# The norm after each expert: passes into a tile of its own, small products four steps late, 14 weight slots instead of 15

## The chip, the cores and the metric

One Trainium2 chip, one NeuronCore of it. The metric is the device time of one execution in microseconds (us). The time before is 2308.57 us, the median of 3 runs (2307.85 to 2309.63).

## The reference, cut to what matters

```
h = concat(meta, x)                       # 16 + 1024 tokens of 2048
h = layer_norm(h, ln_in_g, ln_in_b)       # the input norm
mix = hybrid_mixer(h, ...)                # input projection, convolution and pooling heads, output projection
h = layer_norm(ALPHA*h + mix, ln_mix_g, ln_mix_b)
# mixture of experts: every token goes to 2 of 32 experts
y[t] = sum over its two experts e of gate[t, e] * (silu(h[t] @ w_gate[e]) * (h[t] @ w_up[e])) @ w_down[e]
out  = layer_norm(ALPHA*h + y, ln_ffn_g, ln_ffn_b)[16:]

def layer_norm(x, g, b):
    mu = mean(x); xc = x - mu
    return xc * rsqrt(mean(xc * xc) + 1e-5) * g + b      # over the 2048 columns of a row
```

Each expert has 12 MB of weights (w_gate and w_up 2048x512 each, w_down 512x2048, float32), 32 experts 384 MB.

## The kernel before, in words

The first part (to about 1084 us) normalises the input rows, projects them with float32 numbers that are split into a high and a low half (three products for one), runs the convolution and the pooling, projects the result and routes every token. `ln_stats`, `ln_aggr`, `ln_scale` and `ln_block` are the input norm, on two or three tiles of 128 rows at a time (`PAIRS`); `ln_step` spreads the norm of the next pair over the steps of the present one. Its `aggr` makes mean and reciprocal root on DVE, in fourteen small operations (a bit trick and three Newton steps, all at L262).

The second part (from about 1084 us) goes through the 32 experts in a fixed order. Tokens are sorted by expert; an expert's rows stand in blocks of 32, 64, 96 or 128 rows. A block of up to 64 rows is **narrow** (tile `xgn`): each row is folded over 4 (32 rows) or 2 (64 rows) groups of partitions, so that the block fills 128 partitions. A **wide** block (tile `xgw`) has a row in a partition. An expert has 16 G steps (gate and up products, `gu`) and 8 D steps (down products, `down`). Its weights are 12 units of 1 MB; a step uses half a unit. The list `steps` interleaves experts: the first 8 G steps of the next expert stand ahead of the D steps of this one. SP issues the loads of the units into a ring of 15 slots (10 `er`, 3 `e2a`, one `e2c`, one `e2d`); a slot is loaded again when its unit has been used.

In the step loop each step issues its matmuls (L1482 records all of them), then one advance of what is spread over steps:

- `chain`: the generator `hidden` of the expert whose G steps have ended. ACT makes silu and copies the up sums, DVE multiplies (`sg`, L1572), `YX` = 3 steps later PE transposes `sg` (L1578), and the D steps use it (`hth`). For a 32-row part DVE first adds two halves (`od`, L1502).
- `x_next`: PE transposes of the next expert's rows (L1537), copied to `xt` or `xn` by DVE or ACT (L1539).
- `norm_next`: one advance of the norm at the head of the queue `norms`.

At an expert's last D step `y_out` adds the sums to the block's rows (L1599, L1604, L1615, L1617). Then `rows_out` calls `send` (POOL writes the partial rows to `yd`, L1412), queues the block's norm, sets DVE's `flags` of the next expert (L1636 to L1650) and, `PVS` = 2 steps later, `sums_in` fetches the next expert's partial rows.

`norm`, the function most changed, is on DVE: `bn_stats` (L1668), `bn_aggr` (L1671), then for a narrow block two small products on PE that join the groups of partitions of a row: the mean with `lmv` (L1680) and the variance with `lve` (L1687), each `MATMUL ms<-..,pc`. PE takes its instructions in order, so a step's weight matmuls behind a small product wait with it. Behind it come eight Newton operations and eight **passes** over 512 columns each, in pairs: L1709 takes off the mean and multiplies by the gain, L1710 multiplies by the reciprocal root and adds the offset, both in place in `xgw` or `xgn`. POOL then scatters the block's rows to the output (`out_dram`, L1412). An advance of the norm does one pair of passes, and passes wait until `LNS` = 7 steps behind `rows_out`. A block's place (`xg`) is free for the gather of a later block 8 steps behind the norm's end. The very last norm (`gb` given) has its rows folded by four, so that two passes (L1702, L1703) do it.

Of the kernel before, what the change touches and what calls it, by code (L numbers as in the profile page):

```python
# [57 lines left out]
NE2 = {"a": 3, "c": 1, "d": 1}  # L58

FIRST, FIRST2 = ("a", "a", "a", "c", "d", "x"), ("er", "er", 0, 1)  # L60
# [19 lines left out]
PVS, LNS = 2, 7  # L80
# [3 lines left out]
def trunk_kernel(ctx, tc, xcat, gin, bin_, grow, brow, w_in, b_in, conv_w, conv_b, cln_g, cln_b,  # L84
# [208 lines left out]

    def ln_aggr(tiles):
        c0, c1 = CI[tiles[0]], CI[tiles[-1]] + 1
        aggr([LST[i] for i in tiles], xstat[:, 0, c0:c1], xstat[:, 1, c0:c1])
# [379 lines left out]
    def ln_step(n, g):  # L676
        if n == 0:
# [4 lines left out]
        f = g * 8 // len(GROUPS[n])  # L682
        if (g + 1) * 8 % len(GROUPS[n]) or n + 1 == len(PAIRS):
            return
        nx = PAIRS[n + 1]
        if f == 0:
            ln_stats(nx[-2])
        elif f == 2:
            if nx[0] == 0:
                ln_stats(0)  # L690
            ln_stats(nx[-1])
        elif f == 4:
            ln_aggr(nx)
        elif f in (5, 6, 7):
            for c in ((0,), (1,), (2, 3))[f - 5]:
                ln_scale(nx, c)
# [15 lines left out]
    ln_aggr((1, 2))  # L712
    T0 = []
# [634 lines left out]
    e2["d"] = pool("e2d", NE2["d"])  # L1348
# [6 lines left out]
    lnp = pool("lnp", 3)  # L1355
# [149 lines left out]
    class Block:  # L1505


        def __init__(self, start, n):
            self.start, self.n = start, n
# [45 lines left out]
        def hidden(self):  # L1555
# [12 lines left out]
            for part, (g_, u_) in both.items():  # L1568
# [61 lines left out]
        def flags(self):  # L1630
# [11 lines left out]
            v.scalar_tensor_tensor(ix[:m, 1:2], es[:m], -float(NONE), ef[:m, 1:2], op0=OP.mult, op1=OP.add)  # L1642
            if self.f == 1:
# [15 lines left out]
        def norm(self, into=None, gb=None, wait=lambda: True, idx=None):  # L1659

            f, v = self.f, nc.vector
            m, nseg = self.m if f == 1 else P, 4 // f
            xg, y = self.xg, self.xg if into is None else into
# [3 lines left out]
            for c in range(nseg):  # L1667
                v.bn_stats(out=st[:m, c, :], in_=xg[:m, c * 512:(c + 1) * 512])  # L1668
                if c % 2:
                    yield  # L1670
# [5 lines left out]
            else:  # L1676

                yield
# [5 lines left out]
                yield  # L1684
                yield
# [8 lines left out]
            yield  # L1694
            for _ in range(3):
                v.scalar_tensor_tensor(y2, r, nv, r, op0=OP.mult, op1=OP.mult)
                v.scalar_tensor_tensor(r, y2, 1.5, r, op0=OP.add, op1=OP.mult)
            yield
            while not wait():
                yield  # L1700
            if gb is not None:
                v.scalar_tensor_tensor(xg[:, :512], xg[:, :512], nm, gb[0], op0=OP.add, op1=OP.mult)  # L1702
                v.scalar_tensor_tensor(y[:, :512], xg[:, :512], r, gb[1], op0=OP.mult, op1=OP.add)  # L1703
            else:
                for c in range(4):
# [3 lines left out]
                    v.scalar_tensor_tensor(xg[pc, xc], xg[pc, xc], rs[pc, 0:1], lfg[pc, cs], op0=OP.add, op1=OP.mult)  # L1709
                    v.scalar_tensor_tensor(y[pc, xc], xg[pc, xc], rs[pc, 1:2], lfb[pc, cs], op0=OP.mult, op1=OP.add)  # L1710
                    yield
# [14 lines left out]
    next_ent, next_gather = [0], [0]  # L1726
# [124 lines left out]
    for b in POS[0]:  # L1851
        b.flags()
# [11 lines left out]
    now, norms, sums = [0], deque(), deque()  # L1864

    def rows_out(p, n):
# [3 lines left out]
        for b in POS[p]:  # L1870
            b.send()
            t = er_tile() if last else None
            if last:
                assert b.f == 4
            norms.append((b, b.norm(t, (FIN[:, :512], FIN[:, 512:1024]) if last else None,
                                    lambda: last or now[0] >= n + LNS)))
        nc.vector.tensor_scalar(lim[:, r:r + 1], base[:, r:r + 1],
                                float(FBLK[1] if p < len(STAT) else sum(BLOCKS[RANK[p]][-1])), None, op0=OP.add)
        if not last:
            for b in POS[p + 1]:  # L1880
                b.flags()
# [10 lines left out]
    for n, (kind, p, k) in enumerate(steps):  # L1892
        now[0] = n
        while sums and sums[0][0] <= n:
            for b in POS[sums.popleft()[1]]:
                b.sums_in()
# [3 lines left out]
        if kind == "G":  # L1900
# [16 lines left out]
            if k == 15:  # L1917
                while todo:
                    x_next()
                chain.extend((p, b.hidden()) for b in POS[p])  # L1920
# [30 lines left out]
        norm_next()  # L1951
# [5 lines left out]
    while len(norms) > 1:  # L1957
        norm_next()
    while norms:
        norm_next()  # L1960
# [8 lines left out]
    def left_out(it):  # L1969
# [4 lines left out]
        blk = Block(st, P)  # L1974
        blk.en, blk.xg, blk.gb, blk.pds = ent_load(e, st, P), SPARE, PB6[:2], [PB6[2:4], PB6[4:]]
# [3 lines left out]
    with tc.For_i(0, nov, 1) as it:  # L1979
        blk, e = left_out(it)  # L1980
        blk.fetch()
        blk.flags()
# [87 lines left out]
```

## Time and profile before

| what | value |
|---|---|
| median of 3 runs | 2308.57 us (2307.85 to 2309.63) |
| the profiled execution: time / span | 2310.51 / 2308.7 us |
| busy in the span: PE (matmul) | 2053.9 us (89%) |
| PEld (weight loads of PE) | 1187.8 us (51%) |
| DVE / ACT / POOL | 1414.9 (61%) / 652.8 (28%) / 695.3 us (30%) |
| mean granted clock of PE | 0.943 |
| moved by DMA | 606.52 MB, mean 263 GB/s |
| loads of 1 MB weight units, issue to landing | about 10 us each (median of a group) |

A busy PE is one that has matmuls in it, at whatever clock: the granted clock is given beside it, 1.00 for 2.4 GHz. A wait is idle time of an engine, put down to the instruction on another engine, or the DMA, that ended it. The shares are means over very different stages, so the rows below are read by stage. The profiled execution lasted 1.94 us longer than the median of the runs, and 1.81 us longer than its own span.

### The profile page before, as it was taken

The numbers are of one execution on the slowest core, as the hardware profiler recorded it, in microseconds if no ns is written. First come the engines' busy times: TensorE is split into PE (matmuls) and PEld (weight loads), VectorE is DVE, ScalarE is ACT, GpSimd is POOL, SyncE is SP. The second block draws the span as 40 slices with busy tenths as digits, with TensorE's granted clock in tenths as the row PEclk, the third lists the DMA queues.
The fourth block names the chain that finished last, engine by engine and source line by source line (L and its number), as shares of the span: only waits on it lengthen the run. The fifth ranks groups of instructions, "written<-read, shape, count | busy, mean of one in ns | idle before, by whom it ended". The sixth has DMA issues, their size and how long they took to land. (4 is left out here: it accounts for less than half of the span.)

```text
span 2308.7 us, 30565 instructions
## 1 busy us (share of the span) xinstructions
PE 2053.9 (89%) x10899; PEld 1187.8 (51%) x10899; DVE 1414.9 (61%) x2975; ACT 652.8 (28%) x1159; POOL 695.3 (30%) x593
## 2 busy tenths in 40 slices
PE   5899999999999989985789998989878999788993
PEld 4799999978877878764222222223222232222321
DVE  8678677768675795797375536563554354526445
ACT  5634343423343453543111211121111112111111
POOL 5566657635122354374111101110111011101101
PEclk8999999999999999998899999989988999899996
DMA  6211121133667866677999988996899999978992
GB/s 208 90 55 56 56 65 55 56 97 114 213 210 271 277 216 201 225 273 270 410 394 409 391 311 337 402 412 254 351 359 419 407 361 410 403 278 317 388 386 105
DMA packets 141740, 606.52 MB, mean 263 GB/s; under 512 B 29353, under 2 KB 36009, under 8 KB 87477
## 3 DMA queue, kind: packets, MB, share of 16 engines
q1 hardware_dynamic: 122432, 554.11, 63.3%
q0 software_dynamic: 17712, 42.03, 4.9%
q10 hardware_dynamic: 1440, 8.39, 0.9%
q8 instruction: 87, 1.43, 0.3%
q14 instruction: 69, 0.57, 0.1%
HBM read 579.68 MB, written 73.51 MB: 283 GB/s over the span
## 5 line engine op out<-in xcount | busy, mean ns | idle before, releaser
L760 PE MATMUL mm<-hl,whi 128*128 128x256 f32 (+2 forms) x1152 | 359.4, 324 | 0.6 <-POOL hl L349 0.6
L759 PE MATMUL mm<-hh,whi 128*128 128x256 f32 (+2 forms) x1152 | 347.3, 326 | 0.4 <-ACT l L595 0.4
L379 POOL TENSOR_TENSOR wlo<-raw,whi 128x512 fp32r<-128x512 f32 x129 | 175.4, 1360 | 397.2 <-ACT whi L378 336.9
L1482 PE MATMUL mm<-er,xt 128*64 128x512 f32 (+1 forms) x1248 | 272.3, 642 | 0.0
L764 PE MATMUL mm<-hh,wlo 128*128 128x256 f32 (+2 forms) x1152 | 257.9, 323 | 1.9 <-POOL wlo L379 1.8
L378 ACT ACTIVATE whi<-raw 128x512 fp32r<-128x512 f32 x252 | 156.7, 627 | 270.2 <-PE mm L760 132.7
L418 DVE SCALAR_TENSOR_TENSOR ms<-l,cwt,ms 128x512 f32<-128x512 f32 x352 | 232.5, 747 | 0.0
L760 PEld LDWEIGHTS mm<-hl,whi 128*128 128x128 f32 x1152 | 218.9, 190 | 18.7 <-POOL hl L349 1.0
L759 PEld LDWEIGHTS mm<-hh,whi 128*128 128x128 f32 x1152 | 219.2, 190 | 3.4 <-ACT l L595 0.8
L764 PEld LDWEIGHTS mm<-hh,wlo 128*128 128x128 f32 x1152 | 193.6, 190 | 36.9 <-POOL wlo L379 2.8
L1482 PE MATMUL mm<-er,hth 128*64 128x512 f32 (+1 forms) x1016 | 194.6, 619 | 0.0
L1482 PE MATMUL mm<-er,xn 128*64 128x512 f32 (+1 forms) x840 | 168.3, 646 | 1.2 <-DVE xn L1539 1.2
L1240 PE MATMUL mm<-wlo,yh 128*128 128x512 f32 x392 | 157.6, 402 | 8.3 <-DVE wlo L379 8.2
L1239 PE MATMUL mm<-whi,yh 128*128 128x512 f32 x392 | 159.8, 408 | 0.3 <-ACT whi L378 0.3
L1241 PE MATMUL mm<-whi,yl 128*128 128x512 f32 x392 | 156.5, 399 | 0.0
L1482 PEld LDWEIGHTS mm<-er,xt 128*64 128x64 f32 (+1 forms) x1248 | 68.0, 134 | 162.2 <-issue 159.1
L1615 DVE SCALAR_TENSOR_TENSOR xgw<-mm,xgw 64x512 f32<-64x512 f32 x44 | 30.2, 687 | 191.4 <-ACT dt L1614 190.4
L434 POOL TENSOR_TENSOR l<-l,t 128x512 f32<-128x512 f32 x112 | 142.0, 1298 | 0.0
L379 DVE TENSOR_TENSOR wlo<-raw,whi 128x512 fp32r<-128x512 f32 x123 | 104.5, 861 | 58.4 <-ACT whi L378 56.7
L1482 PEld LDWEIGHTS mm<-er,hth 128*64 128x64 f32 (+1 forms) x1016 | 53.9, 130 | 136.5 <-issue 130.5
L1599 DVE SCALAR_TENSOR_TENSOR xgn<-mm,xgn 64x512 f32<-64x512 f32 x40 | 27.5, 688 | 156.1 <-ACT dt L1597 155.8
L1482 PE MATMUL mm<-e2a,xt 128*64 128x512 f32 (+1 forms) x448 | 97.7, 623 | 0.0
(350 smaller groups left out, 3186.1 us busy)
## 6 DMA issues: line engine op xcount, KB each, us to landing
er<-in_w_gu_dram SPq DMA_DIRECT2D x168, 1024.0 KB, 10.2
er<-in_w_dn_dram SPq DMA_DIRECT2D x86, 1024.0 KB, 10.0
e2a<-in_w_gu_dram SPq DMA_DIRECT2D x54, 1024.0 KB, 10.7
raw<-in_w_out_dram SPq DMA_DIRECT2D x70, 512.0 KB, 5.0
raw<-in_w_in_dram SPq DMA_DIRECT2D x56, 512.0 KB, 3.3
e2a<-in_w_dn_dram SPq DMA_DIRECT2D x21, 1024.0 KB, 9.9
e2d<-in_w_gu_dram SPq DMA_DIRECT2D x17, 1024.0 KB, 11.1
t<-in_xcat_dram SPq DMA_DIRECT2D x56, 256.0 KB, 6.1
```

The source lines that it names most:

```text
L378: nc.scalar.activation(h, src, AF.Copy)
L379: self.lo(s).tensor_tensor(l, src, fr(h), op=OP.subtract)
L418: nc.vector.scalar_tensor_tensor(a, src, w, a, op0=OP.mult, op1=OP.add)
L434: nc.gpsimd.tensor_tensor(a, a, t, op=OP.add)
L759: nc.tensor.matmul(o, wh[:, ks], hh[q][:, kk, a0:a1], start=k == 0, stop=False)
L760: nc.tensor.matmul(o, wh[:, ks], hl[q][:, kk, a0:a1], start=False, stop=False)
L764: nc.tensor.matmul(o, wl[:, ks], hh[q][:, kk, a0:a1], start=False, stop=k == 15)
L1239: nc.tensor.matmul(po[t_], a_, wh, start=n == 0, stop=False)
L1240: nc.tensor.matmul(po[t_], a_, wl, start=False, stop=False)
L1241: nc.tensor.matmul(po[t_], b_, wh, start=False, stop=n == 15)
L1482: nc.tensor.matmul(bank[c:c + self.n], lhs(h_)[:, self.r0:self.r0 + self.n], t[:, h_ * 1024 + j * 512:h_ * 1024 + (j + 1) * 512], start=fi ...
L1615: nc.vector.scalar_tensor_tensor(xs, y0, a, xs, op0=OP.mult, op1=OP.add)
```

## The change

- Input norm: the reciprocal root comes from ACT's square root, a DVE reciprocal and one Newton step (new `ln_rstd`), and ACT copies the mean; in `ln_step` both now stand ahead of the step's own evacuation of sums.
- The weight ring loses slot `e2d` (15 to 14 slots); its 8 KB a partition become `lnz`, a tile for the norm.
- The norm's first passes read the block and write `lnz`, the second passes work in `lnz`, and the scatter reads `lnz`. All four first passes come ahead of the four second ones, one pass an advance. The block's place is free 3 steps behind the last first pass. The wait for `LNS` is gone.
- The small products of a narrow block are issued `PRS` = 4 steps behind the operation before them, both of them (0 for the last expert).
- `norm_next` advances up to two norms in turns (the second one only while the first counts its steps), rests while an expert's `sg` has not been issued, and issues the flags in three portions; the fetch of sums is `PVS` = 4 steps behind `rows_out`.

```diff
-NE2 = {"a": 3, "c": 1, "d": 1}
+NE2 = {"a": 3, "c": 1}
-FIRST, FIRST2 = ("a", "a", "a", "c", "d", "x"), ("er", "er", 0, 1)
+FIRST, FIRST2 = ("a", "a", "a", "c", "x"), ("er", "er", 0, 1)
-PVS, LNS = 2, 7
+PVS, PRS = 4, 4
...
+        nc.scalar.activation(sd, mv[:, :, 1], AF.Sqrt, bias=epst)
+        nc.scalar.activation(xstat[:, 0, c0:c1], mv[:, :, 0], AF.Copy)
+        nc.vector.tensor_scalar(ve, mv[:, :, 1], EPS, -0.5, op0=OP.add, op1=OP.mult)
+        LMV[tiles[0]] = ve, sd, xstat[:, 1, c0:c1]
+
+    def ln_rstd(tiles):
+        ve, sd, rs = LMV.pop(tiles[0])
+        nc.vector.reciprocal(rs, sd)
+        nc.vector.tensor_tensor(sd, rs, rs, op=OP.mult)
+        nc.vector.tensor_tensor(sd, sd, ve, op=OP.mult)
+        nc.vector.scalar_tensor_tensor(rs, sd, 1.5, rs, op0=OP.add, op1=OP.mult)
...
+        if nx and f == 4:
+            ln_aggr(nx)
+        if nx and f == 5:
+            ln_rstd(nx)
         if n == 0:
             ln_evac(PAIRS[0], *GROUPS[0][g], T0[g])
...
-    e2["d"] = pool("e2d", NE2["d"])
+    lnz = pool("lnz", 1).tile([P, D], F32, name="lnz")
...
             nc.vector.scalar_tensor_tensor(sg[:m], sg[:m], self.en[:m, 2:3].bitcast(F32), ul[:m],
                                            op0=OP.mult, op1=OP.mult)
+            self.gated = True
...
-                yield
+                yield from until(now[0] + lag)
                 p_ = ms()
                 nc.tensor.matmul(p_[:, 0:1], PIECE[f], mv[:, 0:1], start=True, stop=True)
...
-                yield
-                yield
+                yield from until(now[0] + lag)
                 q_ = ms()
...
-            while not wait():
-                yield
...
-                for c in range(4):
+                for turn, c in [(t_, c) for t_ in range(2) for c in range(4)]:
...
-                    v.scalar_tensor_tensor(xg[pc, xc], xg[pc, xc], rs[pc, 0:1], lfg[pc, cs], op0=OP.add, op1=OP.mult)
-                    v.scalar_tensor_tensor(y[pc, xc], xg[pc, xc], rs[pc, 1:2], lfb[pc, cs], op0=OP.mult, op1=OP.add)
-                    yield
+                    if not turn:
+                        v.scalar_tensor_tensor(y[pc, xc], xg[pc, xc], rs[pc, 0:1], lfg[pc, cs], op0=OP.add, op1=OP.mult)
+                    else:
+                        v.scalar_tensor_tensor(y[pc, xc], y[pc, xc], rs[pc, 1:2], lfb[pc, cs], op0=OP.mult, op1=OP.add)
+                    if (turn, c) == (0, 3):
+                        sent[self.place] = now[0]
+                    yield True
...
-            if sent.get(b.place, -99) + 8 > n or b.f == 1 and n < WSTEP:
+            if sent.get(b.place, -99) + 3 > n or b.f == 1 and n < WSTEP:
...
     def norm_next():
-        if norms and next(norms[0][1], 0) == 0:
-            sent[norms.popleft()[0].place] = now[0]
+        if marks:
+            mark_next()
+        for g in list(norms)[:2]:
+            r = next(g[1], None)
+            if r is None:
+                norms.remove(g)
+            if r is not False:
+                return
...
-        norm_next()
+        if all(c[2].gated for c in chain):
+            for _ in range(1 + (len(norms) > 2)):
+                norm_next()
```

Place 1 is PE's order of instructions at the end of the thirteenth expert (one block of 32 rows; the products on `xt` and `xn` are those of the next expert, with blocks of 128 and 64 rows). `hth` are the last D steps. Before:

```order
L1482 MATMUL mm<-er,hth 32x512 x16
L1482 MATMUL mm<-er,xt 64x512 x4
L1482 MATMUL mm<-er,xn 64x512 x2
L1680 MATMUL ms<-lmv,pc_10490 128x1
L1482 MATMUL mm<-er,xt 64x512 x4
L1482 MATMUL mm<-er,xn 64x512 x2
```

After the change:

```order
L1507 MATMUL mm<-er,hth 32x512 x16
L1507 MATMUL mm<-er,xt 64x512 x4
L1507 MATMUL mm<-er,xn 64x512 x2
L1507 MATMUL mm<-er,xt 64x512 x4
L1507 MATMUL mm<-er,xn 64x512 x2
L1507 MATMUL mm<-er,xt 64x512 x4
L1507 MATMUL mm<-er,xn 64x512 x2
L1507 MATMUL mm<-er,xt 64x512 x4
L1507 MATMUL mm<-er,xn 64x512 x2
L1562 MATMUL ms<-ident,xgn_10332 128x128 x4
L1713 MATMUL ms<-lmv,pc_10453 128x1
```

Between the D end and the first small product stood the matmuls of one step, now those of four steps and a transpose. (The trace counts each of these matmuls twice.)

Place 2 is DVE's order ahead of `sg` of a 32-row expert, the 24th; the norm there is that of the 23rd, a wide block of 96 rows. Before, from the last copy of rows on:

```order
L1709 SCALAR_TENSOR_TENSOR xgw_10344<-xgw_10344,lrs,lfg 96x512
L1710 SCALAR_TENSOR_TENSOR xgw_10344<-xgw_10344,lrs,lfb 96x512
L1502 TENSOR_TENSOR od<-od,mm 64x512
L1709 SCALAR_TENSOR_TENSOR xgw_10344<-xgw_10344,lrs,lfg 96x512
L1710 SCALAR_TENSOR_TENSOR xgw_10344<-xgw_10344,lrs,lfb 96x512
L1709 SCALAR_TENSOR_TENSOR xgw_10344<-xgw_10344,lrs,lfg 96x512
L1710 SCALAR_TENSOR_TENSOR xgw_10344<-xgw_10344,lrs,lfb 96x512
L1572 SCALAR_TENSOR_TENSOR sg<-sg,en,dt 32x512
```

After the change:

```order
L1729 SCALAR_TENSOR_TENSOR lrs<-lve,lrs 96x1
L1740 SCALAR_TENSOR_TENSOR lnz<-xgw_10308,lrs,lfg 96x512 x4
L1527 TENSOR_TENSOR od<-od,mm 64x512
L1597 SCALAR_TENSOR_TENSOR sg<-sg,en,dt 32x512
L1742 SCALAR_TENSOR_TENSOR lnz<-lnz,lrs,lfb 96x512 x4
```

Eight passes stood ahead of `sg` (one pair above the rows shown); now four do, they read `xgw` and write `lnz`, and the other four stand behind `sg`.

Place 3 is DVE's order in the tail, from the last expert's last `y_out` (L1599, L1604) to its `bn_stats`; the passes are those of the second-last expert's last block. Before:

```order
L1599 SCALAR_TENSOR_TENSOR xgn_10367<-mm,xgn_10367 64x512
L1604 SCALAR_TENSOR_TENSOR xgn_10367<-dt,xgn_10367 64x512
L1877 TENSOR_SCALAR lim<-base 128x1
L1709 SCALAR_TENSOR_TENSOR xgn_10366<-xgn_10366,lrs,lfg 32x512
L1710 SCALAR_TENSOR_TENSOR xgn_10366<-xgn_10366,lrs,lfb 32x512
L1709 SCALAR_TENSOR_TENSOR xgn_10366<-xgn_10366,lrs,lfg 32x512
L1710 SCALAR_TENSOR_TENSOR xgn_10366<-xgn_10366,lrs,lfb 32x512
L1709 SCALAR_TENSOR_TENSOR xgn_10366<-xgn_10366,lrs,lfg 32x512
L1710 SCALAR_TENSOR_TENSOR xgn_10366<-xgn_10366,lrs,lfb 32x512
L1668 BN_STATS lst<-xgn_10367 128x6
```

After the change:

```order
L1912 TENSOR_SCALAR lim<-base 128x1
L1721 COPY lmv<-ms 128x1
L1722 TENSOR_SCALAR lve<-lmv 128x1
L1723 TENSOR_SCALAR lgi<-lve 128x1
L1724 TENSOR_SCALAR lrs<-lgi 128x1
L1725 TENSOR_SCALAR lve<-lve 128x1
L1728 SCALAR_TENSOR_TENSOR lve<-lrs,lve 128x1
L1729 SCALAR_TENSOR_TENSOR lrs<-lve,lrs 128x1
...
L1740 SCALAR_TENSOR_TENSOR lnz<-xgn_10331,lrs,lfg 32x512 x4
L1742 SCALAR_TENSOR_TENSOR lnz<-lnz,lrs,lfb 32x512 x4
L1701 BN_STATS lst<-xgn_10332 128x6
```

Six passes stood between; now eleven small operations (four Newton ones are left out above) and eight passes do.

## Rows read from the trace of the kernel before

**Rows 1.** Busy time by stretch: start:end and length in us, busy time (and instructions) of PE, PEld, DVE, ACT and POOL, granted clock of PE, DMA share, GB/s. The first part, and the expert steps.

```profile
85.00:1084.00 999.00, 960.98 (x5192) 818.73 (x5190) 727.10 (x1170) 415.19 (x737) 483.73 (x380) 0.98 0.46 156
1112.00:2272.00 1160.00, 1026.98 (x5326) 317.50 (x5322) 578.74 (x1532) 180.63 (x316) 146.67 (x150) 0.93 0.93 368
```

**Rows 2.** The waits of PE in 1112 to 2272 us, by what ended them: us in sum, how many, the longest. The last line is who waited for the loads of weight units: us, times.

```profile
PE ms L1680 <- DVE lmv L1671: 68.6, 18, 8.9
PE ms L1578 <- DVE sg L1572: 48.4, 15, 11.4
  PEld mm L1482: 6.1, 11
```

**Rows 3.** The timeline of PE at place 1: start us, us, engine, line, operation, the time it had waited and for what.

```profile
1580.73 1.94 PE L1482 MATMUL mm<-er,xt 128*64 128x512 f32 x8
1582.49 1.03 PE L1482 MATMUL mm<-er,xn 128*64 128x512 f32 x4
1587.32 0.56 PE L1680 MATMUL ms<-lmv,pc 128*128 128x1 f32 x2 [3.80 <-DVE lmv L1671]
1587.81 3.68 PE L1482 MATMUL mm<-er,xt 128*64 128x512 f32 x8
```

**Rows 4.** The timeline of DVE at the same time, from the last `y_out` to the operation that the small product waits for.

```profile
1582.21 0.69 DVE L1604 SCALAR_TENSOR_TENSOR xgn<-dt,xgn 64x512 f32<-64x512 f32 x1
...
1586.27 0.69 DVE L1668 BATCH_NORM_STATS2 lst<-xgn 128x6 f32<-128x512 f32 x1
1586.99 0.18 DVE L1671 BATCH_NORM_AGGREGATE lmv<-lst 128x2 f32<-128x6 f32 x1
```

**Rows 5.** Busy time by stretch, as in rows 1, ahead of that wait and behind it.

```profile
1576.00:1579.00 3.00, 3.00 (x26) 0.79 (x26) 0.00 (x0) 0.00 (x0) 0.00 (x0) 1.00 0.24 44
1585.80:1592.70 6.90, 5.38 (x14) 1.98 (x16) 1.85 (x8) 0.00 (x0) 1.79 (x2) 0.51 0.91 353
```

**Rows 6.** Timelines of PE and DVE around the transposes of `sg` (L1578) of the 15th, 17th, 24th and 31st expert, in this order of time: the wait of PE, and for the last three the first of the passes ahead of `sg`.

```profile
1655.91 0.43 PE L1578 MATMUL ms<-ident,sg 32*128 32x32 f32 x4 [2.94 <-DVE sg L1572]
1721.32 1.94 PE L1482 MATMUL mm<-er,xn 128*64 128x512 f32 x8 [1.16 <-DVE xn L1539]
1724.19 0.75 DVE L1709 SCALAR_TENSOR_TENSOR xgw<-xgw,lrs,lfg 128x512 f32<-128x512 f32 x1 [2.92 <-DMA yd<-xgw,to]
1731.46 0.60 PE L1578 MATMUL ms<-ident,sg 32*128 32x32 f32 x4 [8.21 <-DVE sg L1572]
1971.37 0.75 DVE L1709 SCALAR_TENSOR_TENSOR xgw<-xgw,lrs,lfg 96x512 f32<-96x512 f32 x1 [0.48 <-DMA yd<-xgw,to]
1978.75 0.60 PE L1578 MATMUL ms<-ident,sg 32*128 32x32 f32 x4 [11.38 <-DVE sg L1572]
2251.22 0.75 DVE L1709 SCALAR_TENSOR_TENSOR xgw<-xgw,lrs,lfg 128x512 f32<-128x512 f32 x1 [0.86 <-DMA yd<-xgw,to]
2258.62 0.60 PE L1578 MATMUL ms<-ident,sg 32*128 32x32 f32 x4 [10.32 <-DVE sg L1572]
```

**Rows 7.** Busy time by stretch, as in rows 1: the six stretches of 100 us in the expert steps whose DMA share is 0.98 or more.

```profile
1100.00:1200.00 100.00, 81.55 (x376) 28.04 (x380) 53.87 (x181) 11.02 (x19) 16.33 (x16) 0.87 1.00 404
1200.00:1300.00 100.00, 92.89 (x476) 27.11 (x470) 50.85 (x133) 16.65 (x29) 15.33 (x16) 0.95 0.99 396
...
1700.00:1800.00 100.00, 82.65 (x406) 26.47 (x404) 48.84 (x127) 12.06 (x22) 13.59 (x14) 0.88 1.02 419
1800.00:1900.00 100.00, 97.50 (x508) 29.80 (x506) 46.20 (x126) 16.08 (x28) 10.65 (x12) 0.98 0.98 381
1900.00:2000.00 100.00, 80.15 (x468) 21.23 (x470) 53.75 (x138) 19.76 (x34) 15.11 (x15) 0.86 1.01 411
...
2100.00:2200.00 100.00, 90.53 (x456) 31.08 (x450) 60.90 (x159) 14.25 (x25) 14.77 (x14) 0.97 0.98 391
```

**Rows 8.** The waits of DVE's first passes in 1112 to 2272 us (us in sum, how many, the longest), and the DMA issues of the output scatter of wide blocks: count, median us from issue to landing.

```profile
DVE xgw L1709 <- DMA yd<-xgw,to: 18.9, 12, 3.1
out_dram<-xgw,to POOLq DMA_INDIRECT x15, 8.8
```

**Rows 9.** The timeline of the tail, DVE and POOL: the last `y_out`, the last `bn_stats`, the output scatter of the second-last expert's last block, the first of the last two passes.

```profile
2287.31 0.69 DVE L1604 SCALAR_TENSOR_TENSOR xgn<-dt,xgn 64x512 f32<-64x512 f32 x1
2292.89 0.69 DVE L1668 BATCH_NORM_STATS2 lst<-xgn 128x6 f32<-128x512 f32 x1
2293.13 0.99 POOL L1412 DMA_INDIRECT out_dram<-xgn,to  x1 [3.85 <-DVE xgn L1710]
2297.99 0.75 DVE L1702 SCALAR_TENSOR_TENSOR xgn<-xgn,lrs,xgw 128x512 f32<-128x512 f32 x1
```

**Rows 10.** The input norm: two of PE's waits for normalised rows in 0 to 85 us (sum, count, longest), and from DVE's timeline the first and the last of the fourteen or so small operations, of the first two tiles and of a later pair.

```profile
PE mm L322 <- DVE x L302: 14.5, 1, 14.5
PE ms L322 <- DVE l L302: 7.1, 1, 7.1
10.59 0.38 DVE L262 BATCH_NORM_AGGREGATE mv<-st 128x2 f32<-128x24 f32 x2
13.68 0.16 DVE L262 COPY xstat<-mv 128x2 f32<-128x2 f32 x1
66.44 0.38 DVE L262 BATCH_NORM_AGGREGATE mv<-st 128x2 f32<-128x24 f32 x2
75.13 0.16 DVE L262 COPY xstat<-mv 128x2 f32<-128x2 f32 x1
```

More of the change, by code (lines that the diff above doesn't have):

```diff
@@ L676, in ln_step @@
     def ln_step(n, g):
+        f = g * 8 // len(GROUPS[n])
+        nx = PAIRS[n + 1] if (g + 1) * 8 % len(GROUPS[n]) == 0 and n + 1 < len(PAIRS) else None
+        if nx and f == 4:
+            ln_aggr(nx)
+        if nx and f == 5:
+            ln_rstd(nx)
         if n == 0:
@@ L712, in trunk_kernel @@
     ln_aggr((1, 2))
+    ln_rstd((1, 2))
     T0 = []
@@ L1657, in send, with norm, until @@
             scatter(yd, self.to[:, 0:1], self.xg, self.m if self.f == 1 else P, self.f)
-        def norm(self, into=None, gb=None, wait=lambda: True, idx=None):
-            f, v = self.f, nc.vector
+        def norm(self, gb=None, lag=0, idx=None):
+            f, v, y = self.f, nc.vector, lnz
+            def until(t):
+                while now[0] < t:
+                    yield False
             m, nseg = self.m if f == 1 else P, 4 // f
-            xg, y = self.xg, self.xg if into is None else into
+            xg = self.xg
             st = lnp.tile([P, 4, 6], F32, name="lst", tag="lst")
@@ L1725, in trunk_kernel @@
     SPARE = XW[(ring[True] + 2) % NXW]
-    next_ent, next_gather = [0], [0]
+    next_ent, next_gather, now = [0], [0], [0]
     sent = {}
@@ L1851, in trunk_kernel @@
     for b in POS[0]:
-        b.flags()
+        for _ in b.flags():
+            pass
     chain = deque()
@@ L1863, in trunk_kernel @@
     rows = deque()
-    now, norms, sums = [0], deque(), deque()
+    norms, sums, marks = deque(), deque(), deque()
     def rows_out(p, n):
@@ L1871, in rows_out @@
             b.send()
-            t = er_tile() if last else None
             if last:
                 assert b.f == 4
-            norms.append((b, b.norm(t, (FIN[:, :512], FIN[:, 512:1024]) if last else None,
-                                    lambda: last or now[0] >= n + LNS)))
+                norms.append((b, b.norm((FIN[:, :512], FIN[:, 512:1024]))))
+            else:
+                norms.append((b, b.norm(None, PRS)))
         nc.vector.tensor_scalar(lim[:, r:r + 1], base[:, r:r + 1],
@@ L1879, in rows_out, with sums_in, mark_next @@
         if not last:
-            for b in POS[p + 1]:
-                b.flags()
+            marks.extend(b.flags() for b in POS[p + 1])
             sums.append((n + PVS, p + 1))
-    def norm_next():
-        if norms and next(norms[0][1], 0) == 0:
-            sent[norms.popleft()[0].place] = now[0]
+    def sums_in(p):
+        while marks:
+            mark_next()
+        for b in POS[p]:
+            b.sums_in()
+    def mark_next():
+        if next(marks[0], 0) == 0:
+            marks.popleft()
+    def norm_next():
+        if marks:
+            mark_next()
+        for g in list(norms)[:2]:
[4 more added lines that the diff above has]
+                return
     def quads(bs):
@@ L1894, in trunk_kernel @@
         while sums and sums[0][0] <= n:
-            for b in POS[sums.popleft()[1]]:
-                b.sums_in()
+            sums_in(sums.popleft()[1])
         if n % 4 == 2:
@@ L1919, in trunk_kernel @@
                     x_next()
-                chain.extend((p, b.hidden()) for b in POS[p])
+                chain.extend((p, b.hidden(), b) for b in POS[p])
                 if p + 1 < NE:
@@ L1956, in trunk_kernel @@
                     nc.sync.dma_start(FIN[32 * c:32 * c + 32, 512 * i:512 * i + 512], bc(v_, 512 * c, 512, 32))
-    while len(norms) > 1:
-        norm_next()
     while norms:
+        now[0] += 1
         norm_next()
@@ L1974, in left_out @@
         blk = Block(st, P)
+        blk.place = None
         blk.en, blk.xg, blk.gb, blk.pds = ent_load(e, st, P), SPARE, PB6[:2], [PB6[2:4], PB6[4:]]
@@ L1981, in trunk_kernel @@
         blk.fetch()
-        blk.flags()
+        for _ in blk.flags():
+            pass
         blk.send()
```

34 lines of the change are left out of this document (20 added, 14 removed).

## The prediction

> **What bounds the kernel now.** I read by stage. In the first part PE is busy 961 of 999 us at clock 0.98: full, and the change does not touch it except for the input norm ahead of it [rows 1]. The expert steps, 1112 to 2272 us, are another matter: PE is busy 1027 of 1160 us, so it idles 133 us, and its clock is 0.93, while DVE is busy for half of the stretch and ACT and POOL far less [rows 1]. So here the question is what PE waits for, and the waits answer: 68.6 us, 18 times, for `bn_aggr` ahead of a small product; 48.4 us, 15 times, for `sg`; hardly for weights, 6.1 us [rows 2]. Each of these is a full stop, since PE takes its instructions in order: at place 1 PE has one step of matmuls left behind the last D product (1580.73 to 1583.5), stands 3.80 us, and only then goes on with matmuls that had their weights and rows all along [rows 3]. DVE in that time does the rows' last sums, the flags of the next expert, then `bn_stats` and `bn_aggr`, which ends at 1587.17 [rows 4]. The clock pays as well: it is 1.00 ahead of the wait, and 0.51 in the 6.9 us from the wait on, that is the lower level of 1.2 GHz; eight matmuls that took 1.94 us take 3.68 [rows 3, 5].
>
> [...]
>
> The other resource is DMA. In the stage it moves 368 GB/s at a share of 0.93 [rows 1], that is 0.368 x 1160 = 426.9 MB. The nearest thing to a full DMA are the six stretches whose share is 0.98 or more: 404, 396, 419, 381, 411 and 391 GB/s, mean 400 [rows 7]. At 400 GB/s the 426.9 MB need 1067 us. That is a second floor, 93 us under the present length, and it can bind before PE's does.
>
> **The change part by part.**
>
> *Small products four steps late.* Removed: the wait of PE at the first product of each narrow block. At place 1 one step of matmuls lasts 2.8 us (1580.73 to 1583.5) [rows 3]; the chain on DVE from the end of the D product (1580.7) to `bn_aggr` (1587.17) lasts 6.5 us [rows 4]. Four steps of it are 11 us, so the wait goes. Where the next expert's rows are few, a step is shorter, and four of them hold some 4 us of matmuls. I laid PE's new order against the DVE chain for all narrow blocks (4.0 to 5.6 us where the flags now stand behind it): the rest that stays is about 8 us of the 68.6, five of it at the second expert, two at the 24th, and some tenths at the last two. The term is -60. Bounds: if DVE is more often late than its order tells, half of it, -30; all of it is -68.6 [rows 2].
>
> *One pass a step, four ahead, and passes that do not wait for `send`.* At four places a 32-row expert's `sg` stood behind eight passes of 0.75 us. At the 17th expert the first pass waited 2.92 us for the write to `yd`, since it writes `xgw`, which `send` still reads; now all eight passes are behind `sg`, 8.9 us less on DVE, and of PE's 8.21 us some 1.5 stay (`od` and `sg` behind the last matmul): -6.7. At the 24th and 31st four passes stay ahead: 4 x 0.75 = 3.0, plus the DMA waits of 0.48 and 0.86 that only an in-place pass has: -3.5 and -3.9. At the 15th the 2.94 us are about the four passes that move: -2.9 [rows 6]. Sum -17, of 48.4. Bounds: 0, if DVE fills the place with something else, to -35, if the other eleven waits shrink likewise.
>
> *The lost clock.* 7% of 1027 us is 72 us of work lost to the lower level [rows 1]. I share it out by idle time: 77 of 133 us go, but some of the slow stretches behind stages with thin work stay, so I take 38 us for the two together (-32 and -6), a little under 77/133 x 72 = 42. Bounds: 15 and 50. PE's side of the stage is then -60 - 17 - 38 = -115.
>
> *DMA's side.* -93 by the mean of 400 GB/s; 426.9 MB at 419 GB/s are 1019 us, -141; at 381, 1120 us, -40 [rows 7]. PE's -115 is more than DMA's -93, and a stage ends with the later of them, so the term is **-93**.
>
> *One slot less.* 14 units of 1 MB ahead instead of 15. Units land 14 us or more ahead of their use, as the 6.1 us of waiting for weights also say [rows 2]; a slot is worth 1 MB / 400 GB/s = 2.6 us of lead, so on its own it costs nothing: what hides it is that lead. When PE runs faster the lead shrinks, and the 93 us above already contain that DMA then sets the pace.
>
> *Waits that are added.* The first pass writes `lnz`, which the last block's output scatter must have left: 8.8 us from issue to landing [rows 8]. In the new order the next first pass is at least 5 steps behind that scatter, mostly 7 to 23 (a step is about 3 us), so 0 in the stage; what it would cost without that distance is a rival below. The wait of passes for `send`, 18.9 us on DVE [rows 8], is gone. The rest until `sg` is issued and the fetch of sums at 4 steps only move DVE and POOL work within an expert of some 36 us: 0, bounds -5 and +10.
>
> *The tail.* Between the last `y_out` (ends 2288.0) and the last `bn_stats` (2292.89) stood `lim` and six passes, 4.9 us [rows 9]. Now eleven small operations of about 0.2 and eight passes of 0.75 stand there, 8.2: +3.3. The scatter that frees `lnz` was issued at 2293.13 (+0.99), 4.86 ahead of the first of the last two passes at 2297.99 [rows 9]; it stays some 5 ahead of them, and needs 1 us of issue and some 7 to 8 of landing: the pass waits about 2.5 more. Tail **+6**, bounds +3 and +9.
>
> *The input norm.* For the first two tiles DVE spends 10.97 to 13.84 on small operations, on the way to PE's first matmul, which waits 14.5 us [rows 10]. Now five DVE operations and a trip to ACT: about 1.2 us, -1.6. Later pairs took up to 8.5 us (66.82 to 75.29), and PE waited 7.1 us for one [rows 10]; a third of the operations stays, but ACT's root now stands ahead of the step's evacuation, and not every pair is waited for: -1 to -3 for each of three. Sum **-7**, bounds -3 and -12.
>
> The sum against the profiled execution (2310.51 us; its span 2308.7 plus 1.8 around it) is 2310.5 - 93 - 7 + 6 = 2216.5; against the median, 1.9 lower, **2215**.
>
> **The rivals.**
>
> *A. DMA does not bind.* If the loads run at 419 GB/s as in the best 100 us [rows 7], PE's side decides: 2308.6 - 115 - 7 + 6 = 2193. For it: the rate is there in a stretch in which PE stood 17 us. Against it: such stretches come one at a time.
>
> *B. The waits move on.* When the small products no longer stop PE, it comes 60 us sooner to the transposes of `sg` and rows, which depend on the same DVE, or the loads go at 381 GB/s (-40). Half of PE's gain, about -50 with front and tail: 2259. For it: only 17 of the 48.4 us of `sg` waits are accounted for, and full DMA stretches already exist [rows 2, 7]. Against: DVE is half idle in the stage.
>
> *C. Slower, by the one tile `lnz`.* All norms now go through one tile. If each of the 34 blocks' first passes stood behind the scatter before (up to 10 us, issue and landing) with DVE's later work, `sg` and row copies, queued behind them, PE would pay at each; from 3.4 us each, 34 x 3.4 = 116, it eats PE's 115 and what front and tail leave, and at 4 us each the time is 2308.6 + 136 - 116 = 2329. Against it: the distance of 5 or more steps.
>
> *D. DMA is at its ceiling already, no gain.* The stage would keep its 1160 us, and front and tail cancel: 2308. Against it: the same kernel reaches 419 GB/s for 100 us [rows 7]. The Trainium skill has the rule for this (page "DMA: Bandwidth & Descriptors", section "Where 436 GB/s comes from"): HBM gives a core about 358 GB/s. By it 426.9 MB would need an estimated 1192 us, more than the stage has now, and no wait that is removed would pay. The trace's 368 over the stage and 419 in its best stretch contradict the figure.
>
> **How the numbers follow.** Forecast 0.54; A 0.20; B 0.20; C 0.04; D 0.02. The forecast's own range is 2195 to 2240 (DMA at 393 to 408 GB/s). The range goes out to A's 2193 with its upper bounds and to B's: **2170 to 2266**, which leaves the ends of A and B, and C and D, out. About 0.2% (5 us) is what a measurement of this kernel can tell. All of forecast, A and nearly all of B are faster: faster 0.93, same 0.02, slower 0.05 (C, and a hundredth for B with a long tail).
>
> **What would show it.** In the profile after, PE's wait for `lmv` should be near 8 us in sum, `sg` near 31, the stage's clock 0.96 or more, its DMA share 0.98 or more at about 400 GB/s, with PE now waiting for weights (tens of us instead of 6): that is DMA's floor. If weights are not waited for and the stage is shorter than 1060, A; if `sg` or row copies are waited for more than before, B; if DVE's waits for `lnz` sum to more than some 30 us, C. Between the last `y_out` and the last `bn_stats` 8 us. The prediction is wrong most easily in DMA's floor, a rate read from stretches that were not limited by DMA alone, and in the clock, whose 38 us are shared out and not read.

## The result, and the profile after

The changed kernel takes 2218.82 us (median of 4 runs, 2215.88 to 2219.70) against 2308.82 us before: a ratio of 0.9608 (95% interval 0.9591 to 0.9625), 90.0 us less. The forecast was 2215. The profiled execution took 2215.88 us with a span of 2214.0, so it stands 94.7 us under the profiled span before, and its parts can be told apart by two marks that both traces have: the first weight matmul of the expert steps (1107.2 us before, 1105.2 now) and the transposes of the last expert's `sg` (2270.2 before, 2175.1 now). The part ahead of the experts gave 2.0 us, the expert steps 93.2, the tail cost 0.5. The terms were 7, 93 and 6. The profiled execution of before stands 1.9 us above the median of its runs and this one 2.9 us below, which is why the parts add up to more than the 90.0 us between the medians.

The expert steps, busy time by stretch as in rows 1; the stretch lies to the two marks as 1112 to 2272 us did before (4.8 us behind the first one, 1.9 behind the second):

```profile
1110.00:2177.00 1067.00, 994.15 (x5328) 310.63 (x5328) 564.16 (x1532) 180.69 (x316) 146.51 (x150) 0.97 0.99 401
```

1067 us at a DMA share of 0.99 and 401 GB/s: this is the floor of the forecast (1067 at 400) to the digit. Length and rate are one agreement and not two, since the bytes of the stage stayed (427 MB); that DMA is full is told by the share. PE idles 73 us instead of 133, and its busy time fell from 1027 to 994 with the clock at 0.97 instead of 0.93 [rows 1]. What PE waits for in that stretch, what DVE waits for at the norm tile, and who waited for the loads of weight units (us in sum, how many, the longest; the last line without the longest):

```profile
PE ms L1604 <- DVE sg L1597: 20.8, 7, 8.8
PE ms L1713 <- DVE es L1666: 14.5, 2, 12.9
PE ms L1713 <- DVE lmv L1704: 11.9, 2, 8.1
PE ms L1562 <- DVE xt L1564: 11.2, 4, 5.9
PE ms L1719 <- DVE lve L1716: 4.3, 1, 4.3
PE ms L1604 <- DVE lve L1728: 3.0, 1, 3.0
PE ms L1713 <- DVE to L1674: 1.7, 1, 1.7
```

```profile
DVE lnz L1740 <- DMA out_dram<-lnz,to: 46.1, 6, 13.4
```

```profile
  PEld mm L1507: 26.7, 48
```

The small products (L1713, L1719) still cost 32.4 us of 68.6, `sg` (L1604) 23.8 of 48.4 [rows 2]. DVE's waits for the tile `lnz`, which the forecast had at nothing, are 46.1 us, and one lasts 13.4. The weight loads of PE (PEld) wait for units 48 times instead of 11, but PE itself, as far as the modelled ends of its matmuls tell, had work in hand each time: no wait of PE above names a load.

Place 1 went as worked out. The timeline of PE there and DVE's `bn_aggr`, to be held against rows 3 and 4:

```profile
1541.33 3.64 PE L1507 MATMUL mm<-er,hth 128*32 128x512 f32 x32
1544.90 1.94 PE L1507 MATMUL mm<-er,xt 128*64 128x512 f32 x8
1548.54 0.18 DVE L1704 BATCH_NORM_AGGREGATE lmv<-lst 128x2 f32<-128x6 f32 x1
...
1555.36 0.66 PE L1562 MATMUL ms<-ident,xgn 128*128 128x128 f32 x4
1555.85 0.28 PE L1713 MATMUL ms<-lmv,pc 128*128 128x1 f32 x2
1556.06 1.94 PE L1507 MATMUL mm<-er,xt 128*64 128x512 f32 x8
```

DVE's `bn_aggr` ends at 1548.72, seven microseconds ahead of the product; 3.80 us of wait and the stretch at clock 0.51 behind it are gone [rows 3, 5].

The worst place left is the 17th expert's end. POOL's output scatter, DVE's first pass into `lnz` and PE's small product, in order of time:

```profile
1674.16 1.03 POOL L1437 DMA_INDIRECT out_dram<-lnz,to  x1 [0.31 <-DVE sg L1597]
1685.11 0.66 PE L1562 MATMUL ms<-ident,xgn 128*128 128x128 f32 x4
1688.74 2.74 DVE L1740 SCALAR_TENSOR_TENSOR lnz<-xgw,lrs,lfg 128x512 f32<-128x512 f32 x4 [13.43 <-DMA out_dram<-lnz,to]
1698.66 0.56 PE L1713 MATMUL ms<-lmv,pc 128*128 128x1 f32 x2 [12.89 <-DVE es L1666]
```

The scatter of a narrow block left POOL late (its last pass had ended at 1667.20; three gathers and a fetch of sums went ahead of it on POOL), and it landed 14 us later. The next norm's passes, then the last sums, the flags and `bn_stats` of the following block stood behind it on DVE, and PE's small product, four steps late by the order, stood 12.9 us all the same. From 1685 to 1705 PE's clock was 0.57. That is the mechanism of rival C, at its worst place.

### The profile page after: what moved, and what is told of

The parts are those of the page before. It is cut to its first block, busy times and chain, and to the rows that moved or that the text cites. A ratio compares the mean times of both kernels' runs of the same rounds, so it can differ in the third digit from the quotient of the medians.

```text
span 2214.0 us, 30551 instructions
## 1 busy us (share of the span) xinstructions
PE 2019.9 (91%) x10899; PEld 1181.2 (53%) x10899; DVE 1396.4 (63%) x2939; ACT 653.4 (30%) x1167; POOL 695.8 (31%) x593
## 5 line engine op out<-in xcount | busy, mean ns | idle before, releaser
L1507 PE MATMUL mm<-er,xt 128*64 128x512 f32 (+1 forms) x1408 | 288.0, 606 | 0.0
L1507 PE MATMUL mm<-er,hth 128*64 128x512 f32 (+1 forms) x1072 | 200.3, 601 | 0.0
L1507 PEld LDWEIGHTS mm<-er,xt 128*64 128x64 f32 (+1 forms) x1408 | 75.2, 130 | 176.5 <-issue 162.5
L1437 POOL DMA_INDIRECT out_dram<-lnz,to x35 | 34.9, 996 | 259.6 <-DVE lnz L1742 244.6
L1742 DVE SCALAR_TENSOR_TENSOR lnz<-lnz,lrs,lfb 64x512 f32<-64x512 f32 (+3 forms) x136 | 96.8, 741 | 1.7
```

What stands on the lines that cost most here:

```text
L1507: nc.tensor.matmul(bank[c:c + self.n], lhs(h_)[:, self.r0:self.r0 + self.n], t[:, h_ * 1024 + j * 512:h_ * 1024 + (j + 1) * 512], start=fi ...
L1742: v.scalar_tensor_tensor(y[pc, xc], y[pc, xc], rs[pc, 1:2], lfb[pc, cs], op0=OP.mult, op1=OP.add)
```

## The experiments

The runs of the kernel before that were taken beside each set of experiments have medians of 2303.7 to 2308.8 us, so each kernel is told by its difference to those taken beside it; the changed kernel stands at -90.0. The ratios in brackets are 95% intervals.

**The late small products alone.** In the kernel before:

```diff
-PVS, LNS = 2, 7
+PVS, LNS, PRS = 2, 7, 4
...
-                yield
+                for _ in range(PRS):
+                    yield
                 p_ = ms()
...
-                yield
-                yield
+                for _ in range(PRS):
+                    yield
                 q_ = ms()
```

> The kernel before with one edit: both small products of a narrow block are issued four steps behind the operation ahead of them; passes, slots, flags and the input norm as before. Theory 1 (the late products carry most of the gain, and with them alone DMA's floor is not reached): PE's wait at the small products falls from 68.6 us to 20 or less, the lost clock behind it with it, 60 to 85 us less, about 2235 us. Theory 2 (the late products only hand the wait on to the transposes of sg, because in-place passes still stand ahead of it): the sg wait grows from 48 us to 70 or more, gain 30 us or less, 2280 us or more.

2224.5 us, -84.1 (ratio 0.9632, 0.9616 to 0.9648). Theory 1's numbers hold, its clause on DMA does not (below). PE's waits from the first expert matmul to 2200 us:

```profile
PE ms L1578 <- DVE sg L1572: 42.5, 13, 10.5
PE ms L1681 <- DVE lmv L1671: 19.2, 7, 9.9
```

The `sg` wait did not grow. The small products' wait is under 20 (15.6 without the tail's), and 9.9 of that is the second expert's, where the overflow list runs on DVE. This one edit brings all but 6 us of the change. It also brings DMA near its limit: its share in the steps is 0.98 at 396 GB/s (the second row under the next experiment), and PE waits for weights, 2.1 us.

**Everything but the late products.** In the changed kernel:

```diff
-                yield from until(now[0] + lag)
+                yield from until(now[0] + min(lag, 1))
                 p_ = ms()
...
-                yield from until(now[0] + lag)
+                yield from until(now[0] + min(lag, 2))
                 q_ = ms()
```

> The changed kernel with the small products as early as before (one step and two steps behind the operation ahead of them). Theory 1: the other parts (passes into a tile of their own, one pass a step, rest until sg, 14 slots, input norm) bring only 20 to 35 us, 2275 to 2290 us, and PE's wait at the small products is 50 us or more. Theory 2: they bring half of the gain or more, 2265 us or less.

2251.8 us, -56.8 (0.9753, 0.9737 to 0.9770). Theory 1's time is missed, its wait of 50 us or more is met; theory 2's bound holds. The waits in the expert steps:

```profile
PE ms L1713 <- DVE lmv L1704: 35.0, 7, 11.6
PE ms L1604 <- DVE sg L1597: 21.4, 8, 8.8
PE ms L1713 <- DVE es L1666: 13.6, 4, 7.4
PE ms L1713 <- DVE to L1674: 7.9, 5, 2.1
```

The small products cost 56 us here, not far under the 68.6 of before, and the kernel is 57 us faster, so the other parts bring more than half of the gain by themselves. The two halves add up to 141, and together they give 90. Busy time from mark to mark, as in rows 1, of the kernel before, the late products alone, everything else alone, and the changed kernel, tells what is counted twice:

```profile
1107.20:2270.20 1163.00, 1030.38 (x5325) 318.53 (x5324) 581.95 (x1546) 180.06 (x314) 149.38 (x152) 0.93 0.93 369
1108.80:2188.50 1079.70, 1000.66 (x5326) 311.63 (x5326) 580.04 (x1546) 179.91 (x314) 145.79 (x152) 0.96 0.98 396
1103.90:2211.30 1107.40, 1005.64 (x5326) 314.35 (x5325) 567.28 (x1546) 180.02 (x314) 147.07 (x152) 0.96 0.96 388
1105.20:2175.10 1069.90, 997.05 (x5326) 311.45 (x5326) 567.44 (x1546) 179.94 (x314) 149.22 (x152) 0.97 0.99 401
```

PE's busy time falls by 30 and by 25 us with either half alone, and by 33 with both: each half alone already gives back most of the lost clock. Its idle time falls by 54, by 31 and by 60. So of some 46 us that overlap in the steps 21 are clock and 25 are waits. That the fuller DMA takes part of the 25 is the subject of the next experiment; how the others overlap no run tells apart.

**A quarter fewer weight bytes, after and before.**

```diff
-        t = slot()
+        t = slot()[:, :1536]
...
-        w = 2048 // parts
+        w = 1536 // parts
...
-                                 t[:, h_ * 1024 + j * 512:h_ * 1024 + (j + 1) * 512],
+                                 t[:, min(h_ * 1024 + j * 512, 1024):][:, :512],
...
```

> The changed kernel with three quarters of each weight unit loaded (1536 of 2048 columns; the products on the last quarter use the third one again, so PE's work is the same and the expert sums are not the reference's). 96 MB less to load, some 240 us of DMA time at 400 GB/s. Theory 1 (DMA's floor sets the time of the changed kernel): 15 us or more faster than the changed kernel, 2200 us or less, the 2193 of rival A or under it. Theory 2 (PE's own waits set it, DMA is only just fast enough): within 8 us of 2219.

> The kernel before with the same three quarters of each weight unit loaded (PE's work the same, expert sums not the reference's). Both theories take the kernel before to be bound by PE's waits on DVE, so within 8 us of 2309. If it is more than 15 us faster, loads were in the way before, and the reading of the waits is wrong.

The changed kernel falls to 2199.6 us, -109.0, that is 19 us under itself; the kernel before to 2303.1, -5.4 (0.9978, 0.9966 to 0.9990). So the kernel before was hardly held by its loads (5 us, within the 8 expected) and the changed one is, by 19 us. DMA is not all that holds it: 96 MB less are some 240 us of DMA time, and 19 came free. The changed kernel with fewer bytes from mark to mark, to be held against the last of the four rows above, then what its PE and DVE wait for, show by what way:

```profile
1106.60:2157.00 1050.40, 991.36 (x5326) 308.74 (x5325) 566.55 (x1546) 179.72 (x314) 147.94 (x152) 0.97 0.86 317
```

```profile
PE ms L1713 <- DVE es L1666: 12.3, 2, 10.7
PE ms L1713 <- DVE lmv L1704: 8.7, 2, 6.9
PE ms L1562 <- DVE xt L1564: 5.2, 3, 4.1
PE ms L1719 <- DVE lve L1716: 2.1, 1, 2.1
DVE lnz L1740 <- DMA out_dram<-lnz,to: 35.7, 6, 11.4
DVE xgn L1625 <- DMA xgn<-yd,to: 8.5, 2, 7.3
```

Of the 19.5 us, PE's idle time gives 14 and its busy time 6. The small products wait 23 us instead of 32, the row transposes on `xt` 5 instead of 11; on DVE the waits for scatters fall from 46.1 to 35.7 and those for partial sums from 15.4 to 8.5. The waits of PE's weight loads fall too, from 26.7 to 5.2, but none of them ended idle time of PE. So, as far as the trace tells, the full DMA holds up PE less by late weights than by late sums and scatters, whose packets go through the same 16 DMA engines as the loads.

**The input norm alone, in the kernel before** (`ln_aggr`, `ln_rstd` and `ln_step` as in the change).

> The kernel before with the change's input norm alone (square root on ACT, one Newton step on DVE, both ahead of the step's evacuation; two buffers instead of three for the small tiles of the later norm, to make room). The prediction's term says 3 to 12 us less, 7 likely: 2302 us. The profile of the changed kernel, whose expert steps begin 2.0 us earlier than those of before, says 2 us: 2306.5 us.

2304.4 us, -2.9 (0.9988, 0.9974 to 1.0001). That agrees with the trace's 2 us; the 7 lie outside the interval (6 us at most).

**14 slots, in the kernel before.**

```diff
-NE2 = {"a": 3, "c": 1, "d": 1}
+NE2 = {"a": 3, "c": 1}
...
```

> The kernel before with 14 slots instead of 15 (its 8 KB a partition lie idle). Both theories say no change within 5 us, since units land 14 us or more ahead of their use: 2304 to 2314 us. If it is 10 us or more slower, the lead that the ring gives was worth more than its waits showed.

2307.1 us, -0.2 (0.9995, 0.9978 to 1.0012): the slot was worth nothing there.

**Two norm tiles, and 13 slots.** Both kernels have 13 slots; the first uses the room of `e2c` for a second norm tile, the second leaves it idle:

```diff
-            f, v, y = self.f, nc.vector, lnz
+            f, v, y = self.f, nc.vector, (lnz, lnz2)[nrm[0] % 2]
+            nrm[0] += 1
...
```

> The changed kernel with 13 slots and two norm tiles in turns (the slot e2c gives its room to the second tile). Against e8_13_one, which has 13 slots and one tile. Theory C2 (the one tile is what still stops PE: DVE waits 46 us in six places for its scatter, once 13.4 us with 12.9 us of PE behind it): DVE's wait for the scatter falls under 10 us, and the time is 10 to 25 us under that of e8_13_one. Theory D2 (DMA has no lead left to give, what PE gains here it loses to late weights): DVE's wait falls all the same, but the time is within 6 us of e8_13_one.

> The changed kernel with 13 slots and one norm tile (the room of slot e2c lies idle). In the changed kernel the shortest lead of a weight unit over its use was 1.1 us, at the 25th expert. Theory D2 (DMA is at its limit): a slot less is up to 2.6 us of lead less at each such place, PE now waits for weights, 4 to 15 us slower than the changed kernel, 2223 to 2234 us. Theory C2 (PE's waits for DVE set the time and the lead is only used up, not overdrawn): within 4 us of 2219.

One tile: 2225.9 us, -81.4 (0.9639, 0.9612 to 0.9667). Two tiles: 2214.3, -93.0 (0.9597, 0.9574 to 0.9620). Two tiles are worth 11.6 us by the medians; the intervals touch, but the slowest of four runs with two tiles (2219.0) is under the fastest of four with one (2219.3). A slot, worth nothing before, is worth some 8 us now by the medians (90.0 against 81.4), which is not clear of noise (0.9591 to 0.9625 against 0.9612 to 0.9667). C2's number holds for the second tile, D2's for the slot. The waits with two tiles, PE's and then those for the loads:

```profile
PE ms L1714 <- DVE es L1666: 4.5, 1, 4.5
PE mm L1507 <- DMA er<-in_w_dn_dram: 5.0, 4, 2.7
PE mm L1507 <- DMA er<-in_w_gu_dram: 3.8, 6, 1.5
```

```profile
  PEld mm L1507: 63.5, 73
  PE mm L1507: 15.4, 16
```

DVE waits for no scatter any more, PE's 12.9 us near 1686 are 4.5, and PE itself now waits for weights, 15.4 us, against 5.6 with 13 slots and one tile and none in the changed kernel.

**Only wide blocks through the tile, 14 slots; and with the last fetch early.**

```diff
-            f, v, y = self.f, nc.vector, lnz
+            f, v, y = self.f, nc.vector, lnz if self.f == 1 or gb is not None else self.xg
...
-            sums.append((n + PVS, p + 1))
+            sums.append((n + (PVS if p + 2 < NE else 1), p + 1))
```

(the second edit in the second kernel only)

> The changed kernel (14 slots), in which only wide blocks' norms use the norm tile; narrow blocks' passes work in place again, and a narrow block's place is free 8 steps behind the norm's end. Theory C2 (one tile for both kinds is what stops DVE): DVE's wait for the output scatter falls from 46 us to under 15, PE's 12.9 us near 1686 us to 5 or less, 8 to 15 us under the changed kernel, 2204 to 2211 us. Rival: the in-place passes wait for the write of the partial rows instead (18.9 us on DVE before), or late places of narrow blocks delay gathers: 2215 us or more.

> As e9_narrow_inplace, with the fetch of the last expert's partial rows one step behind the write instead of four (in the changed kernel the last sums waited 4.9 us for this fetch). If the tail's chain is last sums, norm, scatter, the wait goes and the time is 3 to 5 us under e9_narrow_inplace. If DVE's passes of the second-last norm fill the place, no more than 1 us.

2217.0 us, -89.7 (0.9615, 0.9598 to 0.9631), and 2214.8, -91.9 (0.9603, 0.9586 to 0.9619). DVE's wait for the scatter fell to 11.3 us in one place, and nothing was gained: near that place PE now waits for the gather of narrow rows, whose place comes free later.

```profile
1664.08 1.12 PE L1562 MATMUL ms<-ident,xgn 128*128 128x128 f32 x4 [4.64 <-DMA xgn<-h1d,ex]
...
1688.57 1.09 PE L1562 MATMUL ms<-ident,xgn 128*128 128x128 f32 x4 [5.10 <-DMA xgn<-h1d,ex]
```

That is the rival of the expectation. The early fetch is worth 2.2 us by the medians, inside the intervals, and so neither of its two numbers is shown. So no kernel here is clearly faster than the changed one; 13 slots with two tiles (0.9597) and the last of these (0.9603) stand beside it within its interval.

**No rest until `sg`.** In the changed kernel:

```diff
-        if all(c[2].gated for c in chain):
-            for _ in range(1 + (len(norms) > 2)):
-                norm_next()
+        for _ in range(1 + (len(norms) > 2)):
+            norm_next()
```

> The changed kernel without the rest of the norms until an expert's sg has been issued. If the rest is what took PE's wait for sg from 48 to 24 us, that wait is back at 40 us or more, 10 to 25 us slower, 2229 to 2244 us. If passes that no longer wait for the write of partial rows did it, the time is within 6 us of 2219.

2238.2 us, -68.5 (0.9705, 0.9686 to 0.9723): 21.5 us slower than the changed kernel. The rest until `sg` matters, as the first number expected has it. PE's wait for `sg`, and the pass that `sg` stands behind at the 17th expert:

```profile
PE ms L1604 <- DVE sg L1597: 45.9, 12, 17.2
```

```profile
1694.23 0.75 DVE L1740 SCALAR_TENSOR_TENSOR lnz<-xgw,lrs,lfg 128x512 f32<-128x512 f32 x1 [15.07 <-DMA out_dram<-lnz,to]
```

Without the rest, a pass that waits 15 us for the tile stands ahead of `sg` on DVE.

**Two tiles and fewer weight bytes.**

> The kernel with 13 slots and two norm tiles (e7_13_two) with three quarters of each weight unit loaded, as in e3_lite_after (PE's work the same, expert sums not the reference's). In e7_13_two PE waits for weights for the first time (11.8 us). If loads are what now holds it (theory D2), the time falls by 22 us or more, to 2192 us or less, more than the 19 us that the changed kernel gained from the same cut. If the loads only slow the small transfers of rows and sums, the time falls by the same 15 to 20 us, 2194 to 2199 us.

2187.0 us, -116.7 (0.9500, 0.9474 to 0.9527): 24 us under the same kernel with all its bytes by the differences, 27 by the medians. That meets D2's bound, and no wait of PE in that trace names a load any more, where 15.4 us did. That the loads hold this kernel more than the changed one (24 against 19 us) is not clear of noise: the intervals of the two kernels with fewer bytes, 0.9474 to 0.9527 and 0.9510 to 0.9542, overlap.

## Why the prediction was right, step by step

**The length of the expert steps, -93: right, and the floor is real, but it does not act as told.** The experiments show both sides. Without a quarter of the bytes the gain is 109 us, and with a second tile too it is 117; the forecast's PE side was -115 in the steps and -116 over the kernel. From mark to mark the steps are 113 us shorter then (1163.0 to 1050.4), 93 with all bytes. So the steps do end with the later of the two, DMA being it by some 20 us: 401 GB/s against the 400 of the six stretches [rows 7]. The sign that I named, waits for weights of tens of us instead of 6, is there by the line it was read from (PEld, 6.1 to 26.7 [rows 2]), but I took that line for stops of PE, and none of these waits ended idle time of PE. The loads are issued sooner and queue: the median landing of a 1 MB unit of the `er` ring rose from about 10 us to 14 (DMA issues of the page of after):

```profile
er<-in_w_gu_dram SPq DMA_DIRECT2D x184, 1024.0 KB, 14.2
```

The lead of units over their first matmul, worked out from the loads whose landing the trace tells (291 of 385 before, 336 after), was 14 us at its shortest before and is 1.1 now, at the 25th expert. The lead was just used up. What reached PE came by sums and scatters at full DMA (fewer bytes: 14 us less idle) and not, as far as the trace tells, by weights; that weights come next is shown by the kernel with two tiles.

**Small products, -60: the mechanism right, the size not.** Measured in the steps -36 (68.6 to 32.4). What failed in this term is the cover: I laid PE's order against a DVE chain of 4.0 to 5.6 us, and that chain has a DMA in it at one place (12.9 us, through `lnz`), and the overflow list at another (8.1, of which I had five).

**`sg`, -17: measured -24.6, and what carries it was put down wrongly.** I put the gain down to passes that stand behind `sg` and wait for no write, and the rest until `sg` down as an added wait of 0 (bounds -5 and +10). Taken away it costs 21.5 us, and PE's wait for `sg` is back at 45.9: the gain hangs on the rest. The longest wait then is 17.2 us, behind a pass that waits for the tile.

**`lnz`, 0 in the stage: wrong.** I counted steps from scatter to first pass (5 or more), as if a scatter left POOL when its step says. Of the six waits the longest had a scatter that stood behind gathers and a fetch on POOL and then took 14 us to land, against 8.8 in the median [rows 8]. The median itself hardly moved (output scatters of the changed kernel, in the steps):

```profile
out_dram<-lnz,to POOLq DMA_INDIRECT x33, 9.2
```

The 46.1 us are over the 30 that I had set as the sign of rival C; C's price, 3.4 us of PE at each of 34 blocks, did not come. The value of a second tile, 11.6 us at 13 slots, is what this term left out.

**The clock, -38: measured -33** (PE's busy time 1027 to 994), and -39 with a quarter fewer bytes (1030 to 991 from mark to mark). **A slot, 0: right for the kernel before (-0.2), not to be taken as a rule:** once the lead is used up, the next slot is worth some 8 us by the medians, and PE waits 5.6 us for weights.

**The input norm, -7: measured -2.0 in the trace, -2.9 alone.** DVE ends its small operations 1.8 us sooner (12.07 against 13.84 [rows 10]), near the 1.6 told:

```profile
10.99 0.17 DVE L309 TENSOR_SCALAR ve<-mv 128x2 f32<-128x2 f32 x1
...
11.91 0.16 DVE L318 SCALAR_TENSOR_TENSOR xstat<-sd,xstat 128x2 f32<-128x2 f32 x1
```

but PE's first matmul starts only 0.9 us sooner, since the wait was for two things and the other one, a weight tile, now ends it:

```profile
13.58 5.39 PE L344 MATMUL mm<-ident,x 128*128 128x128 f32 x24 [13.58 <-DMA raw<-in_w_in_dram]
```

**The tail, +6: measured +0.5.** DVE's timeline, and POOL's last scatter but one:

```profile
2186.30 0.68 DVE L1625 SCALAR_TENSOR_TENSOR xgn<-mm,xgn 64x512 f32<-64x512 f32 x1 [4.94 <-DMA xgn<-yd,to]
2189.03 0.69 DVE L1630 SCALAR_TENSOR_TENSOR xgn<-dt,xgn 64x512 f32<-64x512 f32 x1
2198.18 0.69 DVE L1701 BATCH_NORM_STATS2 lst<-xgn 128x6 f32<-128x512 f32 x1
2198.42 0.99 POOL L1437 DMA_INDIRECT out_dram<-lnz,to  x1 [7.42 <-DVE lnz L1742]
2203.28 0.75 DVE L1732 SCALAR_TENSOR_TENSOR lnz<-xgn,lrs,xgw 128x512 f32<-128x512 f32 x1
```

From the last sums to `bn_stats` 8.5 us, +3.6 as told (+3.3). The last sums come 3.1 us sooner after the last `sg`, which I left out; without the late fetch it would be more, by 4.9 at most. And the last passes wait for no scatter, though it was issued 4.9 us ahead of them: I took the landing of 7 to 8 us from the full stage, and in the tail the DMA share is 0.08. By my own numbers that wait was 3 to 4 us and not 2.5.

**Luck.** Front and tail were missed by 5.0 and 5.5 us in opposite directions, and that they cancel in the total is luck. The forecast of the steps is not, but PE's terms behind it were mis-sized one by one. In rival B half of PE's gain with front and tail is 58 us and not 50, so its time should have been 2250; the range is hardly touched.

## What to carry to other kernels

A small dependent product in the stream of an engine that takes its work in order is moved behind enough other work to cover its whole chain, which is cheap and was worth 84 us here by itself, and 33 on top of the other parts. Before a wait is costed at nothing because it is so many steps away, look whether a DMA is in the chain, from which queue it leaves and how full DMA is then. Two gains on different waits need not add: here each gave back most of the same lost clock, and together they used up the lead of the loads. Work out that floor first, and look for it in the lead and in the landing times, not only in waits for weights.

## What the runs showed of the hardware

DMA kept 401 GB/s over 1067 us at a share of 0.99: what before it reached only in its fullest stretches of 100 us (381 to 419) [rows 7] can be held through the whole stage. The Trainium skill's figure for a core's share of HBM, about 358 GB/s (page "DMA: Bandwidth & Descriptors", section "Where 436 GB/s comes from"), which was rival D, is passed here again: that section halves a stack's 716 GB/s between two cores, and here one core runs. No run here shows two cores.

In the steps the loads of 1 MB into the `er` ring took 10.6 us in the median to land at a share of 0.93, and 14.5 at 0.99. The output scatters took 8.8 us (wide blocks) and 7.6 (narrow ones) at 0.93, and 9.2 at 0.99, with 14.6 for the slowest; one of 32 rows took less than 4.9 in the tail, at a share of 0.08. So the landing time of a transfer is no constant, and the full share lengthened the loads far more than the median scatter.
